# A hybrid decoder layer: TensorE's order in the heads' stage written by hand, in slots between projection matmuls

## The chip, the core and the metric

The kernel runs on one core of one Trainium2 chip. A core has TensorE (PE, matrix products; its weight loads are listed as PEld), VectorE (DVE), ScalarE (ACT), GpSimd (POOL) and SyncE (SP, which here only issues transfers). The metric is the time of one execution on the device in microseconds (us); lower is better.

## What is computed

The reference is one decoder layer on 512 rows of width 2048, all in float32. Cut to what matters:

```python
z = rms_norm(x, g_mix) @ w_in            # [aq | ak | av | rq | rk | rv | rg], 1024 columns each
# group A, 8 heads: causal attention with QK norm and rotary; group B, 8 heads: retention
aq, ak = rotary(rms_norm(aq, q_norm)), rotary(rms_norm(ak, k_norm))
a_out  = softmax(scale * aq @ ak.T + causal) @ av
rq, rk = rotary(rq), rotary(rk) * 128 ** -0.5
r      = (rq @ rk.T * decay[h]) @ rv
r_out  = silu(rg) * rms_norm_per_head(r) * g_ret
x += concat([a_out, r_out]) @ w_o
h2 = rms_norm(x, g_ffn)
x += (silu(h2 @ w_gate) * (h2 @ w_up)) @ w_down
x += (p @ w_ple_proj) * sigmoid(rms_norm(x, g_ple) @ w_ple_gate + b_ple_gate)
```

With two blocks of 256 keys the block selection takes every earlier block, so group A is plain causal attention.

## The kernel before, in words

Every float32 operand is split into a high and a low float32r part (`split`: one ScalarE copy makes the high part `H`, one VectorE subtraction the low part `L`), and a product is three matmuls into one accumulator (`mm3`, lines 62 to 64: H by H, H by L, L by H).

The kernel has three stretches. **First stage** (to about 298 us): `Plain` makes the q and k columns of head pair 0, then three `Group`s make values and gates with a seven-product scheme. One `step` is one unit of 256 rows of weights; `run` walks the steps and extracts (splits) weights two steps ahead. `beside(i)` issues what lies beside step i: loads of chunks of `xT` (`h_chunk`), of the weights `wqk[0]`, and of the first group's weights `w_vg` at steps 2, 3 and 6, four loads at once.

**Heads' stage** (about 298 to 776 us), the one that changes. Heads come in pairs, i = 0 to 3 attention, i = 4 to 7 retention. For each pair the q and k columns are projected by eight units of 24 matmuls (`rows` for attention, `cols` for retention: unit u, then the four accumulators b or f, then two chunks). The four accumulators are the four buffers of the PSUM pool `acc_p`. When a projection is done, `evac` reads each accumulator. For attention it writes `z` (line 606), four squares with sums on ScalarE (line 610), rotary on GpSimd and VectorE, and the normed `z` at line 625. For retention it copies the accumulator to `zr` (line 682), swaps the halves of its partitions by two transfers on ScalarE's queue into `mr` (lines 685, 686), does rotary on VectorE (lines 688 to 690) and splits the result into `qkH`, `qkL`. `zr` and `mr` share four buffers (tag `rm`), which are given out in program order; so do the pieces of `p` (`praw`, line 780) later. `z` and the broadcast `bc` of `load_ropeT` share four buffers (tag `rp`).

Then come the heads: `attend` (transposes of q and k, line 642; scores, softmax; transposes of the weights, line 667; the weighted values, whose copy is line 672) and `retain` (scores times decay, line 713; values, lines 724 and 725; a norm; transposes, line 740; a copy, line 742). The finished pair is turned into the factors of the seven-product scheme (`mixed`), which go straight into a tile `s_o[p]` or through DRAM (`s_mix`). The code asks for pair i's heads before the projection of pair i + 1. The order of every engine's instructions is then laid out by a planner, which walks the program in the order written but lets later instructions go first where earlier ones wait by its own timing; on the chip each engine runs its list in that order and waits where something is not ready.

At the end of the stage the normed input `h` is freed, the tiles `s_o` of four of the seven products take its place and are refilled from DRAM by `back` on ScalarE's queue, and a small projection `w_pp` (four times 24 matmuls) reads `pTH`, split from `praw`. **The rest** (from about 776 us) is `w_o`, the feed-forward part and the gate, all in `Group`s run by `run`.

Of the kernel before, what the change touches and what calls it, by code (L numbers as in the profile page):

```python
# [33 lines left out]
def layer_kernel(ctx, tc, x, xT, pT, g_mix, wqk, w_vg, qk_norm, g_ret, w_ow, g_ffn,  # L34
# [25 lines left out]

    def mm3(o, aH, aL, bH, bL, start, stop, goes_on=False):
        nc.tensor.matmul(o, aH, bH, start=start, stop=False, skip_group_check=goes_on)  # L62
        nc.tensor.matmul(o, aH, bL, start=False, stop=False, skip_group_check=goes_on)  # L63
        nc.tensor.matmul(o, aL, bH, start=False, stop=stop, skip_group_check=goes_on)  # L64
# [16 lines left out]
    def over_partitions(r):  # L81

        tp = tp_p.tile([P, T], F32, name="tp", tag="tp")
        for b in range(NB):
            nc.tensor.transpose(tp[:, b * P:(b + 1) * P], r[:, b:b + 1].to_broadcast([P, P]), ident)
        return tp
# [106 lines left out]
    class Group:  # L193
# [44 lines left out]
        def multiply(self, p, u):  # L238
# [3 lines left out]
            if first:  # L242
                self.bank[k] = [pools["chain"].tile([P, T], F32, name=k + str(b), tag=k + str(b))
                                for b in range(2)]
# [55 lines left out]
    def chunk_of(get, k):  # L300

        tp = tp_p.tile([P, T], F32, name="tp", tag="tp")
        for b in range(NB):
            nc.tensor.transpose(tp[:, b * P:(b + 1) * P], get(b)[:, k * P:(k + 1) * P], ident)
        return tp
# [164 lines left out]
    def beside(i):  # L470
# [30 lines left out]
    acc_p = mix_ctx.enter_context(pool("acc_p", 4, space=PSUM))  # L501
    at_p = mix_ctx.enter_context(pool("at_p", 2, space=PSUM))
# [10 lines left out]
    def weights(src):  # L513
        tags.append(tags.pop(0))
        raw = rawq.tile([P, 2, T], F32, name="raw", tag=tags[0])
        wh = wq.tile([P, 2, T], F32R, name="wh", tag="wh")
        wl = wq.tile([P, 2, T], F32R, name="wl", tag="wl")
        nc.sync.dma_start(raw, src)
        split(wh, wl, raw)
        return wh, wl  # L520

    def rows(units, evac):

        accs = [acc_p.tile([P, T], F32, name="acc", tag="acc") for _ in range(NB)]
        for u, src in enumerate(units):
            wh, wl = weights(src)
            for b in range(NB):
                at = slice(b * P, (b + 1) * P)
                for c in range(2):
                    k = 2 * u + c  # L530
                    H, L = hT[k]
                    mm3(accs[b], H[:, at], L[:, at], wh[:, c, :], wl[:, c, :], k == 0, k == NC - 1)
        for b in range(NB):
            evac(b, accs[b])

    def cols(units, evac):

        accs = [acc_p.tile([P, T], F32, name="acc", tag="acc") for _ in range(4)]
        for u, src in enumerate(units):
            wh, wl = weights(src)  # L540
            for f in range(4):
                at = slice(f * P, (f + 1) * P)
                for c in range(2):
                    k = 2 * u + c
                    H, L = hT[k]
                    mm3(accs[f], wh[:, c, at], wl[:, c, at], H, L, k == 0, k == NC - 1)
        for f in range(4):
            evac(f, accs[f])
# [50 lines left out]
    def qk_attn(i):  # L599
# [33 lines left out]
        else:  # L633
            rows([wqk[i, u] for u in range(NC // 2)], evac)
        return made

    def attend(z, v, j):
        got = []
        for s in range(2):
            tp = tp_p.tile([P, T], F32, name="tp", tag="tp")  # L640
            for b in range(NB):
                nc.tensor.transpose(tp[:, b * P:(b + 1) * P], z[b][:, s, j, :], ident)
            H, L = qk_pair()
            split(H, L, tp)
            got += [H, L]
        qH, qL, kH, kL = got
        PH, PL = p_tiles()
        nc.vector.tensor_scalar(PH[:, 1408:1536], ident, 0.0, None, op0=ALU.mult)
        nc.vector.tensor_scalar(PL[:, 1408:1536], ident, 0.0, None, op0=ALU.mult)
        for qb in range(NB):  # L650
            nk = (qb + 1) * P
            q = slice(qb * P, nk)
            n = max(nk, 256)
            s = at_p.tile([P, T], F32, name="at", tag="at")
            mm3(s[:, :n], qH[:, q], qL[:, q], kH[:, :n], kL[:, :n], True, True)
            nc.vector.tensor_tensor(s[:, q], s[:, q], mask, op=ALU.add)
            mx = stat.tile([P, 1], F32, name="mx")
            nc.vector.tensor_reduce(mx, s[:, :nk], axis=AX.X, op=ALU.max, negate=True)
            nc.vector.tensor_scalar(mx, mx, SCALE, None, op0=ALU.mult)
            pt = ap.tile([P, T], F32, name="pt", tag="pt", bufs=2)  # L660
            sm = stat.tile([P, 1], F32, name="sm")
            nc.scalar.activation(pt[:, :nk], s[:, :nk], AF.Exp, bias=mx, scale=SCALE, accum_out=sm)
            nc.vector.reciprocal(sm, sm)
            nc.vector.tensor_scalar(pt[:, :nk], pt[:, :nk], sm, None, op0=ALU.mult)
            tp = tp_p.tile([P, T], F32, name="tp", tag="tp")
# [92 lines left out]
    for i in range(2 * NPAIR):  # L758
# [4 lines left out]
        if i + 2 != 2 * NPAIR:  # L763
            mixed(i, made)
# [192 lines left out]
```

## Time and profile before

| what | value |
| --- | --- |
| median of 3 runs | 2428.74 us (2426.74 to 2434.04) |
| the profiled execution | 2433.47 us |
| its span, from the first to the last instruction | 2431.7 us |
| PE busy | 2341.2 us, 96% |
| DVE busy | 1957.4 us, 80% |
| ACT busy | 1210.1 us, 50% |

PE's busy time counts matmuls from start to end, and they overlap; a matmul of 512 columns is shown with about 390 ns but the next one starts before it ends. The granted clock (PEclk) is a share of full speed: 1.00 is 2.4 GHz, 0.50 is 1.2 GHz.

### The profile page before, as it was taken

The numbers are of one execution on the slowest core, as the hardware profiler recorded it, in microseconds if no ns is written. First come the engines' busy times: TensorE is split into PE (matmuls) and PEld (weight loads), VectorE is DVE, ScalarE is ACT, GpSimd is POOL, SyncE is SP. The second block draws the span as 40 slices with busy tenths as digits, with TensorE's granted clock in tenths as the row PEclk, the third lists the DMA queues.
The fourth block names the chain that finished last, engine by engine and source line by source line (L and its number), as shares of the span: only waits on it lengthen the run. The fifth ranks groups of instructions, "written<-read, shape, count | busy, mean of one in ns | idle before, by whom it ended". The sixth has DMA issues, their size and how long they took to land.

```text
span 2431.7 us, 29377 instructions
## 1 busy us (share of the span) xinstructions
PE 2341.2 (96%) x10470; PEld 1917.1 (79%) x10470; DVE 1957.4 (80%) x2632; ACT 1210.1 (50%) x1887; POOL 61.8 (3%) x63
## 2 busy tenths in 40 slices
PE   8999999999978998999999999999999999999998
PEld 6788877787867877888888888888878878888777
DVE  6888677766666798789888988889878877789997
ACT  7644534434445565445545554555544433446643
POOL 0000031100000000000000000000000000000000
PEclk9999999998998999999999999999999999999999
DMA  8545633345566766454356434654595676777764
GB/s 321 154 151 189 207 113 117 117 135 157 170 201 242 263 195 270 139 164 141 120 173 191 144 125 145 192 164 137 170 396 171 246 290 208 287 240 240 276 212 121
DMA packets 169283, 467.81 MB, mean 192 GB/s; under 512 B 18736, under 2 KB 31408, under 8 KB 164144
## 3 DMA queue, kind: packets, MB, share of 16 engines
q1 hardware_dynamic: 164992, 455.43, 56.0%
q10 hardware_dynamic: 4144, 10.50, 1.4%
q8 instruction: 82, 1.34, 0.2%
q14 instruction: 65, 0.53, 0.1%
HBM read 356.28 MB, written 105.38 MB: 190 GB/s over the span
## 4 chain that ended last, share of the span: by engine, by line
PE 67%; DVE 9%; DMA 7%; issue 2%; ACT 2%; ACTq 0%; POOL 0%; SPq 0%; DVEq 0%; POOLq 0%
PE Y L63 8%; PE Y L64 8%; PE Y L62 8%; PE Z L63 5%; PE Z L64 5%; PE Z L62 5%; PE X L63 5%; PE X L62 5%; PE X L64 5%; PE acc L62 4%; PE acc L63 4%; PE acc L64 4%; DVE wl L55 3%; DVE raw L70 2%; DMA mr<-zr 2%
## 5 line engine op out<-in xcount | busy, mean ns | idle before, releaser
L54 ACT ACTIVATE wh<-raw 128x1024 fp32r<-128x1024 f32 x726 | 767.5, 1059 | 815.2 <-PE Y L64 287.7
L55 DVE TENSOR_TENSOR wl<-raw,wh 128x1024 fp32r<-128x1024 f32 x726 | 883.7, 1223 | 261.9 <-ACT wh L54 259.8
L70 DVE TENSOR_TENSOR raw<-raw 128x1024 f32<-128x1024 f32 x376 | 455.1, 1223 | 37.6 <-DMA raw<-in_w_gu 15.9
L63 PE MATMUL Y<-wl,s 128*128 128x512 f32 x1080 | 424.7, 393 | 3.2 <-DVE wl L55 3.0
L64 PE MATMUL Y<-wh,s 128*128 128x512 f32 x1080 | 421.1, 390 | 0.0
L62 PE MATMUL Y<-wh,s 128*128 128x512 f32 x1080 | 378.8, 391 | 8.2 <-ACT wh L54 8.2
L63 PE MATMUL Z<-wl,s 128*128 128x512 f32 x752 | 297.8, 396 | 5.2 <-DVE wl L55 5.2
L64 PE MATMUL Z<-wh,s 128*128 128x512 f32 x752 | 294.5, 392 | 0.0
L62 PE MATMUL Z<-wh,s 128*128 128x512 f32 x752 | 265.8, 393 | 2.2 <-DMA s<-h 2.2
L63 PE MATMUL X<-wl,s 128*128 128x512 f32 x656 | 259.0, 395 | 4.8 <-DVE wl L55 4.6
L64 PE MATMUL X<-wh,s 128*128 128x512 f32 x656 | 257.1, 392 | 0.0
L62 PEld LDWEIGHTS Y<-wh,s 128*128 128x128 f32 x1080 | 201.9, 188 | 54.8 <-ACT wh L54 13.2
L63 PEld LDWEIGHTS Y<-wl,s 128*128 128x128 f32 x1080 | 202.7, 188 | 48.1 <-DVE wl L55 6.7
L62 PE MATMUL X<-wh,s 128*128 128x512 f32 x656 | 232.2, 394 | 3.5 <-ACT wh L54 3.5
L64 PEld LDWEIGHTS Y<-wh,s 128*128 128x128 f32 x1080 | 202.9, 188 | 41.0
L63 PEld LDWEIGHTS Z<-wl,s 128*128 128x128 f32 x752 | 142.4, 189 | 38.1 <-DVE wl L55 8.9
L62 PEld LDWEIGHTS Z<-wh,s 128*128 128x128 f32 x752 | 140.9, 189 | 31.8 <-DMA s<-h 2.5
L64 PEld LDWEIGHTS Z<-wh,s 128*128 128x128 f32 x752 | 142.4, 189 | 29.0
L63 PEld LDWEIGHTS X<-wl,s 128*128 128x128 f32 x656 | 124.2, 189 | 33.6 <-DVE wl L55 7.7
L62 PEld LDWEIGHTS X<-wh,s 128*128 128x128 f32 x656 | 124.1, 190 | 30.7 <-ACT wh L54 4.8
L64 PEld LDWEIGHTS X<-wh,s 128*128 128x128 f32 x656 | 124.2, 189 | 25.4
L62 PE MATMUL acc<-h,wh 128*128 128x512 f32 x256 | 101.5, 398 | 4.1 <-ACT zr L682 3.6
(208 smaller groups left out, 2830.3 us busy)
## 6 DMA issues: line engine op xcount, KB each, us to landing
raw<-in_w_gu SPq DMA_DIRECT2D x176, 512.0 KB, 4.3
raw<-in_w_dn SPq DMA_DIRECT2D x88, 512.0 KB, 6.0
a<-o SPq DMA_DIRECT2D x154, 256.0 KB, 2.7
raw<-in_wqk SPq DMA_DIRECT2D x64, 512.0 KB, 3.7
s<-a SPq DMA_DIRECT2D x14, 2048.0 KB, 10.7
raw<-in_w_vg SPq DMA_DIRECT2D x48, 512.0 KB, 5.0
raw<-in_w_ow SPq DMA_DIRECT2D x32, 512.0 KB, 4.3
xin<-x SPq DMA_DIRECT2D x64, 256.0 KB, 5.9
```

The source lines that it names most:

```text
L54: nc.scalar.activation(H, src, AF.Copy)
L55: nc.vector.tensor_tensor(L, src, H.bitcast(F32), op=ALU.subtract)
L62: nc.tensor.matmul(o, aH, bH, start=start, stop=False, skip_group_check=goes_on)
L63: nc.tensor.matmul(o, aH, bL, start=False, stop=False, skip_group_check=goes_on)
L64: nc.tensor.matmul(o, aL, bH, start=False, stop=stop, skip_group_check=goes_on)
L70: nc.vector.tensor_tensor(o, a, b, op=ALU.add)
```

## The change

All matmuls and transposes from the start of the heads' stage to w_o's eighth step are kept in the order in which they are written (`keep_in_program_order`). The order is then written out. A counter `slot` goes up by one before every 12 projection matmuls (`tick`: twice a unit, twice in each quarter of `w_pp`, and once before each of w_o's first steps), and functions registered with `at_slot(n, ...)` run when the counter gets there. `attend` and `retain` no longer do a head; they return its pieces as functions, whose operations are those of before. `heads` puts the pieces of pair i into slots 7 to 18 (attention) or 1 to 15 (retention) after pair i's projection, so into the projection of pair i + 1; those of pair 7 go into `w_pp` and w_o's first steps. The projections of pair 1 to 7 and `w_pp` take their weights from one `stream`, split up to three units ahead. `load_ropeT` stands before pair 4's projection. Pair 6's factors all go through DRAM now. The PSUM of the heads is handed to w_o in two parts: four buffers of `acc_p` to X and Z at w_o's start, two of `at_p` to Y at its step 5. In the first stage the loads of the first group's weights go out one in each step, from steps 3, 6 and 8.

```diff
+    def matmul(*args, **kw):
+        ins = nc.tensor.matmul(*args, **kw)
+        if in_order[0]:
+            tc.keep_in_program_order(ins)
...
-        for at, q in ((2, "11"), (3, "12"), (6, "22")):
-            if i == at:
-                for u in range(4):
-                    groups[0].load(q, u)
+        for at, q in ((3, "11"), (6, "12"), (8, "22")):
+            if at <= i < at + 4:
+                groups[0].load(q, i - at)
...
-    at_p = mix_ctx.enter_context(pool("at_p", 2, space=PSUM))
+    at_p = at_ctx.enter_context(pool("at_p", 2, space=PSUM, side="right"))
+    in_order[0] = True
+    slot = [0]
+    pieces = {}
+    def at_slot(n, fn):
+        pieces.setdefault(slot[0] + n, []).append(fn)
+    def tick():
+        slot[0] += 1
+        for fn in pieces.pop(slot[0], []):
+            fn()
...
+    stream = [wqk[i, u] for i in range(1, 2 * NPAIR) for u in range(NC // 2)] + [w_pp[n] for n in range(NS)]
+    ready = []
+    def weights():
+        while stream and len(ready) < 3:
...
+            split(wh, wl, raw)
+            ready.append((wh, wl))
+        return ready.pop(0)
+    def projection(rows):
         accs = [acc_p.tile([P, T], F32, name="acc", tag="acc") for _ in range(4)]
+        for u in range(NC // 2):
+            wh, wl = weights()
             for f in range(4):
+                if f % 2 == 0:
+                    tick()
...
+    def heads(i, made, v):
+        out = []
+        if i < NPAIR:
+            (turn0, scores0, weights0, result0), (turn1, scores1, weights1, result1) = \
+                [attend(made, v, j) for j in range(2)]
+            plan = ((7, turn0), (8, lambda: scores0((0, 1))), (10, lambda: weights0((0, 1))),
+                    (10, lambda: scores0((2, 3))), (11, turn1), (12, lambda: weights0((2, 3))),
+                    (12, lambda: scores1((0, 1))), (14, lambda: out.append(result0())),
+                    (14, lambda: weights1((0, 1))), (14, lambda: scores1((2, 3))),
+                    (16, lambda: weights1((2, 3))), (18, lambda: out.append(result1())))
+        else:
+            (load0, scores0, normed0, result0), (load1, scores1, normed1, result1) = \
+                [retain(made, v, j, 2 * (i - NPAIR) + j) for j in range(2)]
+            plan = ((1, load0), (5, lambda: scores0((0, 1))), (6, lambda: scores0((2, 3))), (6, load1),
+                    (8, normed0), (9, lambda: scores1((0, 1))), (10, lambda: scores1((2, 3))),
+                    (11, lambda: out.append(result0())), (12, normed1), (15, lambda: out.append(result1())))
+        for n, fn in plan:
+            at_slot(n, fn)
+        at_slot(plan[-1][0], lambda: mixed(i, out))
+
     for i in range(2 * NPAIR):
+        if i == NPAIR:
+            load_ropeT()
+        qk = qk_attn(i) if i < NPAIR else qk_ret(i)
+        heads(i, qk, v_of(i))
+    h_ctx.close()
...
     for n in range(NS):
+        wh, wl = weights()
         accs = [acc_p.tile([P, T], F32, name="acc", tag="acc") for _ in range(NB)]
         for b in range(NB):
+            if b % 2 == 0:
+                tick()
...
+    def take_over(i):
+        if 0 <= i < 10:
+            tick()
+        if i == 5:
+            at_ctx.close()
+            pools["chainY"] = ctx.enter_context(pool("chain3", space=PSUM, side="right"))
+        if i == 8:
+            assert not pieces
+            in_order[0] = False
+            mix_ctx.close()
...
+            for p in "724":
+                nc.sync.dma_start(s_o[p].bitcast(F32), s_mix[p].bitcast(F32))
```

## Rows read from the trace of the kernel before

**Rows 1.** The page: busy time of each engine, with its share of the span and the count of instructions.

```profile
PE 2341.2 (96%) x10470; PEld 1917.1 (79%) x10470; DVE 1957.4 (80%) x2632; ACT 1210.1 (50%) x1887; POOL 61.8 (3%) x63
```

**Rows 2.** PE in order of time at five places: the first projection matmul of the stage, the start of pair 6's projection, the last matmul of pair 7's, the first of w_pp, the first of w_o. Columns: start, length, engine and line, operation, tiles, shape, count, and in brackets idle time before it and what ended that.

```profile
298.32 0.47 PE L62 MATMUL acc<-wh,h 128*128 128x512 f32 x1 [0.38 <-DVE e L67]
...
606.44 0.39 PE L62 MATMUL acc<-h,wh 128*128 128x512 f32 x1
...
715.04 0.39 PE L64 MATMUL acc<-h,wl 128*128 128x512 f32 x1
...
747.37 0.63 PE L62 MATMUL acc<-wh,pT 128*128 128x512 f32 x1
...
775.81 0.40 PE L62 MATMUL X<-wh,s 128*128 128x512 f32 x1
```

**Rows 3.** PE in order of time where nothing holds it up: a head's last matmuls of 384 and 256 columns, four transposes, projection matmuls of 512 columns.

```profile
386.48 0.33 PE L62 MATMUL at<-PH,v 128*128 128x384 f32 x1
387.00 0.28 PE L62 MATMUL at<-PH,v 128*128 128x256 f32 x1
...
387.71 0.60 PE L642 MATMUL tp<-ident,z 128*128 128x128 f32 x4
...
388.38 0.40 PE L62 MATMUL acc<-wh,h 128*128 128x512 f32 x1
...
390.44 0.39 PE L62 MATMUL acc<-wh,h 128*128 128x512 f32 x1
...
392.71 0.39 PE L63 MATMUL acc<-wl,h 128*128 128x512 f32 x1
```

**Rows 4.** PE in order of time at the end of pair 2's projection, up to the start of pair 3's.

```profile
408.19 0.39 PE L64 MATMUL acc<-wh,h 128*128 128x512 f32 x1
...
410.59 0.51 PE L62 MATMUL at<-PH,v 128*128 128x512 f32 x1 [1.25 <-ACT PH L54]
...
416.67 0.79 PE L62 MATMUL acc<-wh,h 128*128 128x512 f32 x1 [0.53 <-ACT m L610]
```

**Rows 5.** Stretches: length, busy time (and count) of PE, PEld, DVE, ACT, POOL, then the granted clock, the share of the DMA engines and GB/s.

```profile
410.00:420.00 10.00, 7.34 (x30) 5.64 (x31) 8.75 (x17) 6.76 (x38) 3.25 (x4) 0.83 0.26 80
470.00:480.00 10.00, 6.68 (x38) 5.09 (x36) 7.37 (x15) 6.76 (x30) 1.58 (x3) 1.00 0.24 75
540.00:570.00 30.00, 22.57 (x90) 17.79 (x89) 21.90 (x54) 13.65 (x31) 0.00 (x0) 0.77 0.42 134
715.00:750.00 35.00, 14.11 (x49) 11.10 (x49) 23.18 (x50) 12.27 (x31) 2.37 (x2) 0.63 0.90 305
400.00:450.00 50.00, 46.68 (x223) 38.38 (x222) 36.46 (x81) 20.56 (x65) 11.80 (x12) 0.97 0.27 85
30.00:35.00 5.00, 0.86 (x4) 0.38 (x2) 0.50 (x1) 0.76 (x2) 0.00 (x0) 0.94 1.03 395
```

**Rows 6.** VectorE in order of time: the first and the last steps of pair 0's `z`.

```profile
309.03 1.29 DVE L606 TENSOR_TENSOR z<-z,sides 128x512 f32<-128x512 f32 x2 [2.61 <-DMA sides<-in_qk_norm]
...
325.01 1.28 DVE L625 TENSOR_TENSOR z<-z,rs 128x512 f32<-128x512 f32 x2
```

**Rows 7.** Groups of instructions from 290 to 760 us: count, busy time and mean ns of one, idle time before.

```profile
L610 ACT ACTIVATE m<-acc 128x128 f32<-128x128 f32 x48 | 12.4, 332 | 0.0
L610 ACT ACTIVATION_READ_ACCUMULATOR m<-acc 128x1 f32 x48 | 11.8, 266 | 0.0
```

**Rows 8.** ScalarE in order of time: the four copies `zr` of pair 5's accumulators.

```profile
600.15 0.60 ACT L682 ACTIVATE zr<-acc 128x512 f32<-128x512 f32 x1 [0.55 <-PE acc L64]
...
603.91 0.60 ACT L682 ACTIVATE zr<-acc 128x512 f32<-128x512 f32 x1
...
610.32 0.58 ACT L682 ACTIVATE zr<-acc 128x512 f32<-128x512 f32 x1
...
616.03 0.58 ACT L682 ACTIVATE zr<-acc 128x512 f32<-128x512 f32 x1
```

**Rows 9.** The chain that ended last, its pieces that are swaps of halves: start, length.

```profile
601.35 6.29 DMA mr<-zr
614.40 4.14 DMA mr<-zr
...
730.01 12.66 DMA mr<-zr
```

**Rows 10.** ScalarE in order of time after pair 7's projection: the first and the third copy `zr`, and the first refill of `s_o`.

```profile
708.98 0.60 ACT L682 ACTIVATE zr<-acc 128x512 f32<-128x512 f32 x1 [0.55 <-PE acc L64]
...
717.28 0.33 ACTq L748 DMA_DIRECT2D s<-mix  x1
...
719.94 0.58 ACT L682 ACTIVATE zr<-acc 128x512 f32<-128x512 f32 x1
```

**Rows 11.** VectorE in order of time: the rotary of pair 7's third accumulator.

```profile
731.41 0.69 DVE L690 TENSOR_TENSOR zr<-zr,mr 128x512 f32<-128x512 f32 x1
```

**Rows 12.** The tile `praw`: its transfers (duration of the issue, first and last start), their time to landing, and, from the waits of SyncE's queue from 700 to 750 us, what its issue waited for.

```profile
L780 SPq DMA_DIRECT2D praw<-in_pT x2: 332/332/333, 736.7 to 741.5; - x2
DMA to landing us min/median/max: 3.4/5.2/7.0
SPq L780 <- DMA s<-mix: 6.0, 2, 4.3
```

**Rows 13.** SyncE's queue in order of time in the first stage.

```profile
16.76 4.92 SPq L204 DMA_DIRECT2D raw<-in_w_vg  x6
```

More of the change, by code (lines that the diff above doesn't have):

```diff
@@ L633, in qk_attn @@
         else:
-            rows([wqk[i, u] for u in range(NC // 2)], evac)
+            for b, acc in enumerate(projection(True)):
+                evac(b, acc)
         return made
     def attend(z, v, j):
[L638 to L645, printed above, removed]
@@ L670, in attend, with turned @@
-        o = weighted(v, (PH, PL), j)
-        a = ev_tile("A", name="o")
-        nc.scalar.activation(a, o, AF.Copy)
-        return a
+        got, pts, ps = [], {}, []
+        def turned():
+            for s in range(2):
+                tp = tp_p.tile([P, T], F32, name="tp", tag="tp")
+                for b in range(NB):
+                    transpose(tp[:, b * P:(b + 1) * P], z[b][:, s, j, :])
+                H, L = qk_pair()
+                split(H, L, tp)
+                got.extend([H, L])
@@ new lines, in weights_turned @@
+        def weights_turned(qbs):
+            if not ps:
+                ps.extend(p_tiles())
+                for t in ps:
+                    nc.vector.tensor_scalar(t[:, 1408:1536], ident, 0.0, None, op0=ALU.mult)
+            PH, PL = ps
+            for qb in qbs:
+                nk = (qb + 1) * P
+                tp = tp_p.tile([P, T], F32, name="tp", tag="tp")
+                for kb in range(qb + 1):
+                    transpose(tp[:, kb * P:(kb + 1) * P], pts[qb][:, kb * P:(kb + 1) * P])
+                blocks = lambda t: t.rearrange("p (k c) -> p k c", c=P)[:, qb:4 * qb + 1:3, :]
+                split(blocks(PH), blocks(PL), tp[:, :nk].rearrange("p (k c) -> p k c", c=P))
@@ L676, in qk_ret, with result @@
+        def result():
+            o = weighted(v, ps, j)
+            a = ev_tile("A", name="o")
+            nc.scalar.activation(a, o, AF.Copy)
+            return a
+        return turned, scores, weights_turned, result
     def qk_ret(i):
@@ L693, in evac @@
             made.append((H, L))
-        cols([wqk[i, u] for u in range(NC // 2)], evac)
+        for f, acc in enumerate(projection(False)):
+            evac(f, acc)
         return made
@@ L738, in retain, with load @@
-        tp = tp_p.tile([P, T], F32, name="tp", tag="tp")
-        for qb in range(NB):
-            nc.tensor.transpose(tp[:, qb * P:(qb + 1) * P], r[:, qb], ident)
-        a = ev_tile("A", name="r")
-        nc.scalar.activation(a, tp, AF.Copy, scale=gr[:, h:h + 1])
-        return a
+        own = {}
+        def load():
+            own["dec"] = ap.tile([P, P + T], F32, name="dec", tag="dec")
+            nc.sync.dma_start(own["dec"], decay_c[h])
+            own["sg"] = rp_tile("sg", (P, NB, HD))
+            nc.sync.dma_start(own["sg"], sgd[:, :, h * HD:(h + 1) * HD])
@@ L746, in back, with result @@
+        def result():
+            tp = tp_p.tile([P, T], F32, name="tp", tag="tp")
+            for qb in range(NB):
+                transpose(tp[:, qb * P:(qb + 1) * P], own["r"][:, qb])
+            a = ev_tile("A", name="r")
+            nc.scalar.activation(a, tp, AF.Copy, scale=gr[:, h:h + 1])
+            return a
+        return load, scores, normed, result
     def back(p, pairs):
         nc.scalar.dma_start(s_o[p][:, pairs].bitcast(F32), s_mix[p][:, pairs].bitcast(F32))
-    qk, v = qk_attn(0), v_of(0)
@@ L884, in layer_kernel, with before @@
     b_at = steps.index((groups[-2], "3", 0))
-    run(lambda i: load_bias() if i == b_at else None)
+    def before(i):
+        take_over(i)
+        if i == b_at:
+            load_bias()
+    run(before)
 def _constants():
```

212 lines of the change are left out of this document (91 added, 121 removed).

## The prediction

> **What bounds the kernel now.** I read the page first: PE is busy 96% of the span [rows 1], so only PE's lost time can be won. Next PE in order of time. With nothing in the way, projection matmuls start 2.27 / 10 = 0.227 us apart, those of 384 columns 0.17, of 256 columns 0.118, and four transposes take 0.67 - 0.227 = 0.44 [rows 3]. At that pace the heads' stage needs: seven projections and w_pp, 1440 matmuls, 327 us; eight attention heads of 18 transposes (2.0) and two products of 3 x (0.227 + 0.17 + 2 x 0.118) = 1.9, so 5.8 each, 46.6; eight retention heads of 1.9 for scores, 20 x 0.118 = 2.4 for values, 0.44 for transposes, 4.7 each, 37.8; four transposes more. Sum 412 us. The stage lasts from 298.32 to 775.81 [rows 2], 477.5 us, so **65.5 us are lost in it**, and that is what this change can work on.
>
> Where? At the ends of the attention projections: between the last matmul at 408.19 and the next projection at 416.67 there are 15 transposes (1.7) and 12 matmuls (1.9), so 8.5 - 0.2 - 3.6 = 4.7 are lost [rows 4], and at this one the granted clock then reads 0.83 over 10 us, 1.7 more; at the third it reads 1.00 [rows 5]. Three such tails: about 17. Around pair 4's rotary table, 540 to 570, 7.4 idle and a clock of 0.77 (up to 6.9 more) [rows 5]: about 14. At the end, from pair 7's last projection matmul at 715.04 to w_pp's first at 747.37 [rows 2], 32.3 us hold 5.7 us of head work: 26.6 lost, and about 2 more at half clock behind it [rows 5]: 28.5. The rest, 6, lies in short waits.
>
> **The change, part by part.** No operation is added or removed, save pair 6's extra way through DRAM (2 MB more, off PE's path). What changes is who waits. An order written by hand never lets a later matmul pass a waiting one; each term below is PE's wait at a place, since every matmul of the stage is queued behind it.
>
> *Tails.* Both heads' pieces lie inside the projection; the last, slot 18, is 1.9 us of work behind the next projection's first 12 matmuls. The tails' 17 go. What comes is the hand-over of accumulators: four squares with sums, 4 x (0.332 + 0.266) = 2.4 us of ScalarE for each accumulator [rows 7]. The first accumulator is done 4.9 us before the projection ends, the four take 9.6, two weight splits of 1.06 lie between, so the last is free some 7 us after the end, and is wanted at 12 + 6 matmuls + 1.9 = 6.0. I take 1.5 for each of three (0 to 4): **4.5**.
>
> *Pair 0.* Its pieces start in slot 7, after three units: 298.32 + 72 x 0.227 = 314.7 [rows 2, 3]. Its last `z` is ready at 325.01 + 1.28 = 326.3, and that chain does not hang on PE: it starts when the table `sides` lands at 309.0 [rows 6]. The planner fed projection matmuls past the transposes there; by hand nothing may pass, so PE waits 11.6, and after such a wait comes a stretch at half clock like the 1.7 above: **13.4** (9 to 15).
>
> *Rotary table.* The 14 go, since the table is made 45 us before it is wanted. But its transposes hold one of two buffers of `tp_p` until `bc` can be written, and `bc` is the fifth user of four `rp` buffers: it waits for pair 3's slot 11. Until then transposes share one buffer; each second one waits for a copy (0.6) and a subtraction (0.69 [rows 11]) and their hand-overs. Two at 1.5, one at 1: **4** (1.5 to 6).
>
> *Retention.* `zr` and `mr` have four buffers, so the third copy waits until the first swap is through. In the trace the third copy starts 10.2 us after the first, the fourth 12.1 after the second [rows 8]; the swap is the larger part of it (6.29 [rows 9]). Before, PE went round this: pair 6's projection started at 606.44 [rows 2] while the third copy came at 610.3. By hand the third accumulator is wanted 2.7 us after the projection's end T. Its first copy starts at T - 3.8 (18 matmuls before the end), so the third is done at T - 3.8 + 10.2 + 0.6 = T + 7.0, a wait of 4.3, and the fourth at T + 10.3 against T + 8.4, 1.9 more: 6.2, and 7.9 with a half-clock stretch. With the shorter swap of 4.14 [rows 9] and VectorE free it is about 2.3. Transfers that ran beside that swap lie elsewhere in the new order, so I take 5.2 for each of three: **15.5** (7 to 24).
>
> *The end.* w_pp's first matmul needs `praw`, whose buffers come after pair 7's third accumulator in the same four. Before, that one's copy started 719.94 - 715.3 = 4.6 after T, its rotary ended at 732.1, 16.8 after T [rows 10, 11], and `praw` was issued at 736.7 and 741.5, SyncE's queue held up 6.0 by refills [rows 12]. The copy came that early because the first accumulator was done at T - 6.3 [rows 10]; now it is T - 3.8, so third copy T + 6.4, rotary T + 18, landing 5.2 later [rows 12], copy and subtraction: w_pp at T + 25, with nothing before it, as its matmuls stand ahead of pair 7's pieces. With half clock after it **27** (21 to 33; the latter if the queue is held as before). So 28.5 become 27. The third swap here runs beside the refills from 717.28 [rows 10], and the fourth took 12.66 against 4.14 in the quiet [rows 9]. The Trainium skill (DMA: Bandwidth & Descriptors, Issuing engines are not separate DMA queues) says that transfers issued by different engines end on the same DMA engines and interleave; the trace agrees, with the 12.66. If the queues were separate, the quiet 4.14 would hold and the end would be 22, the sum 5 lower; I keep 27.
>
> *Slots.* Each piece has one to three slots of 2.7 us behind the one that feeds it. About 80 pieces at 0.06: **5** (2 to 15). *w_o's start*, where pair 7's heads now meet w_o's additions on VectorE: **2** (0 to 8).
>
> *First stage.* Six `w_vg` loads go out at 16.76 in one row [rows 13], with the DMA engines full, and at 30 to 35 PE has 0.86 of 5 us, waiting for `h` [rows 5]; about 8 are lost there. Spread out, the chunks of `xT` come first: **-5.5** (-8 to 0).
>
> Sum of waits: 4.5 + 13.4 + 4 + 15.5 + 27 + 5 + 2 = 71.4, against 65.5; less 5.5: +0.4. So the profiled execution's 2433.5 stays, and since the median lies 4.7 under it, **2429**. The two holes and tails that go (31) are paid back in waits at fixed places.
>
> **The rivals.** *Covered, faster.* The swap is quick without its neighbours (9 for the three instead of 15.5), `praw` comes at T + 20 (22), pair 0 costs 10, slots 2, the table 2, the front gives 7.5: 3 + 10 + 2 + 9 + 22 + 2 + 1 = 49, so 49 - 65.5 - 7.5 = -24: 2405; halfway, about 2412. For: none of the three swaps in rows 9 is typical of a quiet queue except 4.14. Against: pair 0's wait is dated by a load.
>
> *Late pieces, slower.* ScalarE and VectorE still run the planner's order, made by its own timing; each piece that comes late stops PE, where before other matmuls stood in between. VectorE is busy 36.5 of 50 us in this stage [rows 5], and with periods of 57 instead of 61.6 us over 78%. Price: 80 pieces at 0.3 us are 24 instead of 5: 2448. It decides from 0.15 us a piece. Against: PE's whole list of waits before is short.
>
> *The clock.* Short waits in a row at the accumulators throw PE to half clock again and again: half clock followed one tail and not another of the same gaps [rows 5]. At three attention hand-overs, the rest of the retention ones and four slots, 1.7 each: +15, 2444. The Trainium skill (TensorE: Matmul & The Clock Gate, A second HAM failure mode: psum-queue depth-cycling) describes this: micro-idles between groups, as PE goes round its PSUM banks, make the clock swing, and the throughput falls; the 0.83 behind the tail agrees, the 1.00 does not.
>
> **How the numbers follow.** Forecast (even) 0.32; covered 0.33; late pieces 0.27; clock 0.08. What the measurement tells from no change is 0.3%, 7.3 us: faster 0.33 (all of covered), same 0.31, slower 0.36. The forecast's own range is 2419 to 2439; taking in the others, **2407 to 2452**.
>
> **What would show it.** Right: PE waits near 315 for `z` for over 9 us; PE waits on `zr` at the start of the projections of pairs 5 to 7, 2 to 6 us each; no hole at 540 to 570; the projections of attention pairs follow each other with under 2 us lost; nothing on PE for 20 us or more ahead of w_pp. Wrong: w_pp starting within 15 us of pair 7's projection (then some 10 faster), waits of over 0.5 us at most pieces (slower), or a different loss after 860, where I expect none.

## The result

The changed kernel takes 2453.01 us (median of 6 runs, 2444.98 to 2454.19); the kernel before, run beside it, 2432.71 (6 runs). The ratio is **1.0079, with a 95% interval of 1.0059 to 1.0099**: about 19 us slower. My forecast, no change, did not come. Slower came, to which I had given 0.36, against 0.33 for faster and 0.31 for no change. On the 2428.74 from which I forecast, 1.0079 are 2448: outside the forecast's own range (2419 to 2439), near the slow end of the whole one (2407 to 2452). The median itself is 1 us beyond that end, with a kernel before that took 4 us more here.

The page of the changed kernel, to be read against [rows 1]: busy time of each engine. PE's share fell by a point, and its work is the same.

```profile
span 2452.4 us, 29384 instructions
...
PE 2335.7 (95%) x10470; PEld 1914.4 (78%) x10470; DVE 1957.7 (80%) x2632; ACT 1210.5 (49%) x1887; POOL 59.8 (2%) x63
```

PE's waits in the changed heads' stage (290 to 780 us), by line and by what ended them: sum, count, longest. L64 is now every matmul of a product, L69 every transpose.

```profile
PE acc L64 <- ACT pT L54: 31.5, 1, 31.5
PE acc L64 <- ACT zr L720: 11.6, 5, 3.0
PE tp L69 <- DVE z L646: 9.6, 2, 5.3
PE tp L69 <- DVE qkL L55: 5.5, 2, 3.0
PE at L64 <- DVE qkL L55: 2.5, 1, 2.5
PE at L64 <- ACT qkH L54: 1.5, 1, 1.5
```

There are few rows. The first four are fixed places that I had named; the last two, scores that wait for q and k, I had priced only among the slots. Two rows under 1 us follow; all come to 63 us. The same view of the kernel before adds up to 40.

Stretches of the changed kernel that answer to [rows 5]: length, busy time (and count) of PE, PEld, DVE, ACT, POOL, granted clock, DMA share, GB/s.

```profile
310.00:330.00 20.00, 10.27 (x36) 7.81 (x35) 15.18 (x24) 4.70 (x19) 7.80 (x7) 0.66 0.24 75
335.00:485.00 150.00, 149.96 (x750) 126.45 (x749) 118.52 (x278) 69.23 (x215) 34.16 (x36) 1.00 0.38 120
490.00:525.00 35.00, 28.83 (x133) 23.57 (x132) 19.39 (x47) 12.50 (x28) 0.00 (x0) 0.90 0.41 128
540.00:570.00 30.00, 23.68 (x100) 18.67 (x99) 21.14 (x38) 11.18 (x20) 0.00 (x0) 0.94 0.64 187
660.00:690.00 30.00, 25.79 (x101) 20.40 (x100) 21.05 (x35) 12.38 (x21) 0.00 (x0) 0.83 0.52 148
725.00:770.00 45.00, 13.53 (x51) 10.57 (x50) 16.58 (x28) 12.33 (x23) 0.00 (x0) 0.66 0.80 283
```

For 150 us, over three attention hand-overs, PE never stops and its clock reads 1.00. That is what the change was good for. Before and behind it stand the holes.

To add this up I take the length of a stretch less the matmuls that start in it, each at its pace [rows 3] (0.227 us for 512 columns, 0.176 for 384, 0.118 for 256, 0.114 for a transpose). The paces are rounded here; by them a cell comes out up to 0.7 lower, differences between kernels hardly change. This lost time holds waits and half clock alike. Here it is for all kernels; the experiments follow below.

```
lost us   pair 0   attention  table    hand-overs  end      then
          290-335  335-485    485-525  525-700     700-780  780-1010
before      2.1      17.5       0.1      17.8 (a)    29.3     16.9
after      13.9       1.2       9.7      26.3        34.2     17.2
e_free      1.4      13.7       0.2      16.1        27.8     16.6
e_front    13.0       1.2       8.3      24.0        36.3     16.7
e_pair0     0.8      10.5       9.9      24.0        33.6     17.0
e_bc       12.3       1.4       0.6      24.5        33.8     17.9
e_zr       13.2       1.4       8.3      22.0        27.8     17.0
e_late     13.7       1.4       9.8      26.2        26.4     16.7
e_ret3     14.1       1.2       8.8      16.9        29.4     16.6
e_end      12.8       1.2       8.3      22.3        25.6     18.2
e_hbest     3.1      13.8       0.8      15.6        24.9     16.2
e_fbest     3.0      10.1       0.3       3.6        21.5     23.0
e_fback     2.1      11.2       0.2      14.9        31.1     14.1
e_spread    1.9       8.5       0.2       6.6        12.7     23.0
(a) 14.6 of it is the rotary table's hole, 525 to 580
```

Before to after: 66.8 lost become 85.3 from 290 to 780, +18.5. The first stage gives 1.8 (23.4 to 21.6 lost), which is within what the traces differ by (see e_front). Of the profile's 20.7 us of difference 4 lie elsewhere: some 6 more are lost behind 2000 us, some 2 fewer between 1010 and 2000.

### The profile page after: what moved, and what is told of

Read it like the earlier page. It is cut to its first block, busy times and chain, and to the rows that moved or that the text cites. A ratio compares the mean times of both kernels' runs of the same rounds, so it can differ in the third digit from the quotient of the medians.

```text
span 2452.4 us, 29384 instructions
## 1 busy us (share of the span) xinstructions
PE 2335.7 (95%) x10470; PEld 1914.4 (78%) x10470; DVE 1957.7 (80%) x2632; ACT 1210.5 (49%) x1887; POOL 59.8 (2%) x63
## 4 chain that ended last, share of the span: by engine, by line
PE 66%; DVE 11%; DMA 7%; issue 2%; ACT 1%; ACTq 0%; SPq 0%; DVEq 0%
PE Y L64 22%; PE Z L64 15%; PE X L64 14%; PE acc L64 11%; DVE wl L55 4%; DVE raw L82 3%; PE at L64 3%; PE tp L69 2%; DMA h<-o 1%; DMA mr<-zr 1%; DMA xin<-x 1%; DVE t L79 1%; ACT wh L54 1%; DMA mix<-o 1%; DVE o L55 1%
## 5 line engine op out<-in xcount | busy, mean ns | idle before, releaser
L64 PE MATMUL Y<-wh,s 128*128 128x512 f32 x2160 | 680.9, 391 | 7.2 <-ACT wh L54 7.2
L64 PEld LDWEIGHTS Y<-wh,s 128*128 128x128 f32 x2160 | 405.3, 188 | 94.0 <-ACT wh L54 11.0
L64 PE MATMUL Z<-wh,s 128*128 128x512 f32 x1504 | 475.0, 391 | 2.3 <-DMA s<-h 2.1
L64 PE MATMUL Y<-wl,s 128*128 128x512 f32 x1080 | 425.2, 394 | 3.5 <-DVE wl L55 3.3
L64 PE MATMUL X<-wh,s 128*128 128x512 f32 x1312 | 416.8, 393 | 5.3 <-ACT wh L54 5.3
L64 PEld LDWEIGHTS Z<-wh,s 128*128 128x128 f32 x1504 | 282.3, 188 | 60.7 <-DMA s<-h 2.3
L64 PE MATMUL Z<-wl,s 128*128 128x512 f32 x752 | 297.4, 396 | 6.2 <-DVE wl L55 6.2
L64 PEld LDWEIGHTS X<-wh,s 128*128 128x128 f32 x1312 | 248.1, 189 | 58.4 <-ACT wh L54 7.2
L64 PE MATMUL X<-wl,s 128*128 128x512 f32 x656 | 259.1, 395 | 5.8 <-DVE wl L55 5.7
L64 PEld LDWEIGHTS Y<-wl,s 128*128 128x128 f32 x1080 | 203.2, 188 | 48.4 <-DVE wl L55 7.3
L64 PE MATMUL acc<-h,wh 128*128 128x512 f32 x512 | 166.3, 407 | 11.6 <-ACT zr L720 11.6
L64 PEld LDWEIGHTS Z<-wl,s 128*128 128x128 f32 x752 | 141.7, 188 | 40.7 <-DVE wl L55 12.4
L64 PEld LDWEIGHTS X<-wl,s 128*128 128x128 f32 x656 | 124.1, 189 | 34.4 <-DVE wl L55 8.8
L64 PE MATMUL acc<-wh,h 128*128 128x512 f32 x384 | 124.9, 396 | 0.4 <-DVE e L79 0.4
L64 PEld LDWEIGHTS acc<-h,wh 128*128 128x128 f32 x512 | 98.2, 197 | 33.1 <-ACT zr L720 14.0
L64 PE MATMUL acc<-h,wl 128*128 128x512 f32 x256 | 103.2, 403 | 0.0
L64 PEld LDWEIGHTS acc<-wh,h 128*128 128x128 f32 x384 | 73.2, 191 | 15.8 <-issue 0.8
L54 ACT ACTIVATE o<-t 128x256 fp32r<-128x256 f32 x149 | 56.6, 409 | 45.3 <-DVE t L79 35.6
L64 PE MATMUL acc<-wl,h 128*128 128x512 f32 x192 | 75.7, 394 | 0.0
```

What stands on the lines that cost most here:

```text
L54: nc.scalar.activation(H, src, AF.Copy)
L64: ins = nc.tensor.matmul(*args, **kw)
```

## The experiments

My theory was that each hole has a cause of its own, a wait that the order written by hand cannot go round. The rival was that the lost time is conserved: that another engine or the transfers set it, and it comes back at the next place. Every ratio is to the kernel before on the same chip.

**e_free: the slots without the order.** One line goes.

```diff
-    in_order[0] = True
```

> The changed kernel with its slots, streams and pools, but the tensor engine's order in the heads' stage left to the planner instead of held as written. Theory (the order held by hand makes the engine stand at a late piece, pair 0 and the hand-overs of pairs 4 to 6, with projection matmuls ready behind it): the loss of 13 us in pair 0 and of 25 at the hand-overs shrinks to a third or less, the end stays at 30 or more, time 2425 to 2438. Rival (the waits come from buffers and latencies that any order meets): the same places lose as much, time 2449 to 2456.

Measured: 2430.07 us, 0.9983 (0.9974 to 0.9993). Its four longest rows of waits from 290 to 780:

```profile
PE at L64 <- ACT qkH L54: 28.5, 4, 23.0
PE acc L64 <- ACT zr L719: 2.8, 1, 2.8
PE acc L64 <- DVE wl L55: 2.4, 1, 2.4
PE tp L69 <- DVE qkL L55: 1.9, 2, 1.4
```

The theory's time came. The slots, streams and pools with the planner's order are as fast as the kernel before, 0.2% faster; **keeping the order by hand costs 1.0079 - 0.9983, about 23 us**. The waits on `z` and most of those on `zr` are gone, since PE goes round them. In detail it is not as I wrote: the hand-overs of pairs 4 to 6 still lose 16 of 26, the end falls to 27.8, and the attention hand-overs lose 13.7 again, against 1.2. The order by hand wins 12.5 there and loses 12.5 in pair 0, 9.5 at the table, 10 at the hand-overs and 6 at the end. One reservation: with that line gone the planner lays out the lists of ScalarE and VectorE anew too (in the two traces they run in a different order), so the 23 us are the price of the fixed order together with what the planner makes of the rest; no run parts the two.

**e_front: the first stage's loads as before**, all else changed.

```diff
-        for at, q in ((3, "11"), (6, "12"), (8, "22")):
-            if at <= i < at + 4:
-                groups[0].load(q, i - at)
+        for at, q in ((2, "11"), (3, "12"), (6, "22")):
+            if i == at:
+                for u in range(4):
+                    groups[0].load(q, u)
```

> The changed kernel with the loads of w_vg of the first stage back at the steps where the kernel before has them, all four at once. Theory (these loads gave 1.8 us of the 5.5 that I forecast): projection 1 starts 1 to 3 us later than at 296.5, time 2453 to 2457. Rival (the moved loads gave the 5.5 and something else in the first stage took the rest): projection 1 starts 4 to 7 us later, 2457 to 2460.

Measured: 2448.59, 1.0063 (1.0045 to 1.0081), no slower than with the new loads, and projection 1 starts 0.4 us later. Both fail: no gain from the moved loads can be told. With the new loads the first stage loses between 21.6 and 24.3 us in the traces here, with the old ones 22.0 and 23.4.

**e_pair0: pair 0's pieces five slots later.**

```diff
+        held = 5 if i == 0 else 0
         for n, fn in plan:
-            at_slot(n, fn)
+            at_slot(n + held, fn)
```

> The changed kernel with pair 0's twelve pieces held five slots later and nothing else. Theory (pair 0's z are late for their slot, and the stall and the clock behind it cost 13.4 us between 310 and 330): both waits on z go, the tensor engine keeps full clock there, and the time falls by 9 to 13 us, to 2440 to 2444 (1.003 to 1.005 of before). Rival (the lost time is only moved: pair 0's last pieces now meet pair 1's first in projection 2, and vector and scalar engine are no earlier with them): waits of the same size on tiles of pair 0 or 1 between 340 and 380, time 2449 to 2455.

Measured: 2448.02, 1.0065 (1.0043 to 1.0088); by the times alone not to be told from the changed kernel. The trace is clear: 13.1 us go at the old place and 9.3 come back in the next 150. PE's waits there, 310 to 400:

```profile
PE at L64 <- ACT pt L686: 4.5, 1, 4.5
PE tp L69 <- DVE pt L688: 1.4, 2, 0.8
PE tp L69 <- DVE qkL L55: 0.8, 1, 0.8
```

Five slots later, pair 0's softmax falls into the hand-over of projection 1. The engine behind the longest of these waits is VectorE, not ScalarE, which had made the squares by then and stood idle for VectorE's maximum `mx`:

```profile
356.86 0.37 ACT L686 ACTIVATE pt<-at,mx 128x128 f32<-128x128 f32 x1 [2.86 <-DVE mx L683]
```

From 340 to 370 VectorE is busy for 26.64 of 30 us, with the norm and rotary of projection 1's `z` among it. For this hole the rival is right, for some two thirds of it.

**e_bc: the broadcast row in a buffer of its own.**

```diff
-        bc = rp_tile("bc")
+        bc = ap.tile([P, 2, T], F32, name="bc", tag="pT")[:, 0, :]
```

> The changed kernel with the broadcast row bc in a buffer of its own (the pT tile's, idle until the end), nothing else. Theory (bc waits for a buffer of the z of pair 3, so one of the two tp tiles is held and the transposes of head 0 wait, 9.8 us with the clock between 490 and 525): the two waits of the transposes on qkL go, the loss there falls to 1 to 3 us, time down by 6 to 9, to 2444 to 2447. Rival (the transposes wait for the vector engine's split itself, not for the buffer): the waits stay, time 2451 to 2455.

Measured: 2443.83, 1.0053 (1.0038 to 1.0067). The two waits are gone, and where the clock read 0.90 (above) this stretch now shows

```profile
490.00:525.00 35.00, 34.74 (x178) 29.27 (x177) 24.76 (x65) 15.49 (x36) 0.00 (x0) 1.00 0.48 152
```

The loss falls from 9.7 to 0.6 and does not come back: theory. The time is just below the theory's, and its interval overlaps that of the changed kernel; it is the trace that decides.

**e_zr: copies 2 and 3 of each retention projection elsewhere**, in the idle pT tile.

```diff
-            z = rm_tile("zr")
+            if f == 2:
+                late.append(ap.tile([P, 2, T], F32, name="zr", tag="pT"))
+            z = rm_tile("zr") if f < 2 else late[0][:, f - 2, :]
```

> The changed kernel with the last two of the four copies zr of each retention projection in the idle pT tile instead of the four rm buffers. Theory (the hand-overs cost 8 to 9 us each, 25 together, because copies 2 and 3 wait for the buffers of 0 and 1, hold the accumulators, and the tensor engine falls to half clock): the five waits of acc on zr (11.6 us) go, the hand-overs shrink to 2 to 5 us each, and the time falls by 10 to 18, to 2435 to 2443. Rival (the scores wait for q and k, which the swaps' latency sets): the wait moves from the accumulators to at or tp on qkH or qkL in the next slots, time 2448 to 2455.

Measured: 2443.07, 1.0049 (1.0029 to 1.007). PE's waits from 525 to 705, over the three hand-overs:

```profile
PE at L64 <- DVE qkL L55: 7.4, 3, 3.7
PE at L64 <- ACT qkH L54: 4.6, 2, 2.6
PE acc L64 <- ACT zr L723: 0.3, 1, 0.3
```

The accumulators' waits went from 11.6 to 0.3 and the scores' waits on q and k from 4.0 to 12.0: the rival's transfer, to the letter. The hand-overs lose 22.0 instead of 26.3, not the theory's 6 to 15. The time is at the slow edge of the theory's all the same, since most of it was won elsewhere, at the end (27.8 instead of 34.2), where `praw` no longer comes behind those copies in the same four buffers.

**e_ret3: on top of e_zr, the pieces later**: pairs 4 and 5 by three slots, pair 6 by one.

```diff
+        held = {4: 3, 5: 3, 6: 1}.get(i, 0)
```

> The kernel of e_zr (copies 2 and 3 in the pT tile), and the pieces of pairs 4 and 5 three slots later, those of pair 6 one slot later. Theory (with the accumulators free, slot 5 is too early for the first scores: q and k come some 9 us later than their slot): the waits of at on qkH and qkL go at the hand-overs of pairs 4 and 5 (near 550 and 610), where 5 to 7 us each are lost in e_zr, down to 1 or 2 us, and shrink by less than half at that of pair 6; time 8 to 12 below e_zr's 2443, 2431 to 2435. Rival (the vector engine is the limit: each hand-over's loss is its backlog, and comes back at a later slot): waits of the same sum between 550 and 600 and between 610 and 660, time 2440 to 2445.

Measured: 2439.01, 1.0028 (1.0016 to 1.0041); some 4 us won, not 8 to 12. By stretch, e_zr's losses 6.2, 7.6 and 8.2 (525 to 580, 580 to 640, 640 to 700) become 1.7, 4.4 and 10.8. At pair 4 no wait on q or k is left. At pair 5 what is left is a wait of 2.1 for a weight. At pair 6, moved by one slot only, there stand

```profile
PE at L64 <- ACT qkH L54: 4.8, 1, 4.8
PE at L64 <- DVE qkL L55: 2.3, 1, 2.3
```

Where the pieces moved three slots the loss shrank by 4.5 and 3.2, with no such wait at a later slot of the same projection; there the theory holds for the mechanism. Of these 7.7 us the third hand-over lost 2.6 again and the end 1.6. Whether more than one slot would have mended the third was not tried.

**e_late: the refills of w_o's factors behind the last swap** on ScalarE's queue.

```diff
+            swap[0] = nc.scalar.dma_start(m[half:], z[:half])
...
+        with tc.issue_after(swap[0].ins):
+            nc.scalar.dma_start(s_o[p][:, pairs].bitcast(F32), s_mix[p][:, pairs].bitcast(F32))
```

> The changed kernel with the refills of w_o's factor tiles queued on the scalar engine behind the last swap of pair 7, nothing else. Theory (seven refills of half a megabyte each, issued from 731 on, hold ACT's queue and the DMA engines, so the third swap goes out at 738.5 instead of 733 and lands in 8 instead of 4 us): w_pp's first matmul comes 6 to 12 us earlier than 759, time 2441 to 2447, if the refills are not needed sooner. Rival (they are: w_o's first steps wait for them): w_pp starts earlier, but X or Z wait for s after it by as much, time 2450 to 2458.

Measured: 2441.87, 1.0045 (1.0029 to 1.006). The chain at the end, changed kernel first, then e_late: start, length, what.

```profile
731.67 6.69 DMA mix<-o
...
738.46 0.47 ACTq L723
...
739.00 8.13 DMA mr<-zr
...
748.55 0.70 DVE zr L728
...
749.30 9.12 DMA praw<-in_pT
...
759.13 13.19 PE acc L64 x48
```

```profile
728.74 4.24 DMA mix<-o
...
738.13 2.44 DMA mr<-zr
...
741.99 0.70 DVE zr L730
743.10 8.49 DMA s<-mix
751.99 0.64 ACT pT L54
752.67 14.20 PE acc L64 x48
```

The swap lands in 2.44 us instead of 8.13, PE's wait falls from 31.5 to 22.5, and nothing comes back behind it. So the refills stretched the swap, and the theory's time came. The third swap was issued less early than I had written: at 737.6 here, which is 7.4 us behind projection 7's end (730.2) instead of 10.8. And now the refills hold the queue ahead of pT's split.

**e_end: on top of e_zr, pT loaded and split during projection 7.**

```diff
+    def load_pT():
+        for k in range(2):
+            both = [rp_tile("pT", dt=F32R) for _ in range(2)]
...
+            raw = ap.tile([P, T], F32, name="praw", tag="pt", bufs=2)
+            nc.sync.dma_start(raw, pT[k * P:(k + 1) * P, :])
+            split(*both, raw)
...
+        if i == 2 * NPAIR - 2:
+            plan += (13, load_pT),
```

> The kernel of e_zr, and pT loaded and split during projection 7, into the four rp buffers that the heads of pair 6 have left, so that w_pp waits neither for the rm buffers nor for the loads; sg of pair 7 then comes after w_pp. Theory (the hole at the end is the chain of the last q and k, the loads of pT behind it and their split; w_pp itself needs none of it): w_pp's first matmul within 3 us of projection 7's last, the 27 us lost there in e_zr fall to 5 to 15 (the scores of pair 7 and the refills of w_o are next in the order), time 12 to 22 below e_zr, 2421 to 2431. Rival (the refills set the end: w_o cannot start before its factors are in, and they start only when h is done with): the tensor engine waits as long after w_pp instead, for s from the refills, time 2438 to 2445.

Measured: 2440.78, 1.0043 (1.0031 to 1.0054), 2 us under e_zr instead of 12 to 22. The hole only changed its name. PE's waits from 715 to 800, and below them ScalarE's queue in order of time:

```profile
PE acc L64 <- ACT pp L871: 17.3, 4, 8.9
```

```profile
735.71 11.20 ACTq L806 DMA_DIRECT2D s<-mix  x8
746.95 0.63 ACT L54 ACTIVATE qkH<-zr 128x512 fp32r<-128x512 f32 x1 [10.67 <-DMA s<-mix]
```

w_pp starts at once, but its accumulators are emptied by ScalarE, which for 11 us issues refills. The rival's time came, by another way than it said: not w_o waits, but ScalarE. That its queue is what sets the end does not follow from this trace, as e_hbest shows next.

**e_hbest, e_fbest, e_fback: the fixes together.** e_hbest joins e_bc, e_zr and e_end, `held = {0: 3, 4: 3, 5: 3, 6: 1}`, and issues the refills from GpSimd; e_fbest is the same without the order by hand; e_fback is e_free with GpSimd's refills alone.

```diff
-        nc.scalar.dma_start(s_o[p][:, pairs].bitcast(F32), s_mix[p][:, pairs].bitcast(F32))
+        nc.gpsimd.dma_start(s_o[p][:, pairs].bitcast(F32), s_mix[p][:, pairs].bitcast(F32))
```

> Order still held by hand, with the edits of the earlier runs together (bc in the pT tile, copies 2 and 3 of zr there too, pieces of pairs 0, 4 and 5 three slots later and of pair 6 one, pT loaded and split during projection 7) and the refills of w_o's factors issued from GpSimd's queue. Theory (each of the losses has its own cause, and at the end it is the refills' issue that holds the scalar engine's queue for 11 us in e_end): pair 0 loses 7 instead of 13 us, the tables 1 instead of 10, the hand-overs 12 to 15 instead of 25, the end 10 to 15 instead of 34; sum 45 to 50, so 2403 to 2410. Rival (w_o cannot start before its factors are in, whoever issues them): the end keeps 25 or more, waits of X on s, 2420 to 2428.

> The kernel of e_hbest with the tensor engine's order left to the planner. Theory (with buffers and refills out of the way little is left to wait for, and the planner's order fills it): 10 to 25 us below e_free's 2430, 2405 to 2420, within 6 us of e_hbest. Rival (the planner's own estimates place its holes, and they do not go with these buffers): the losses at the hand-overs near 340, 400, 460 and 540 and at the end stay, 2425 to 2432.

> The kernel of e_free (planner's order) with the refills of w_o's factors on GpSimd's queue, nothing else. Theory (the refills' issue holds the scalar engine's queue at the end): the 27 us lost there fall to 15 to 21, time 2418 to 2425. Rival (their transfers are the limit, not their queue): 2427 to 2432.

Measured: e_hbest 2428.81, 0.9992 (0.9982 to 1.0001); e_fbest **2407.94, 0.9903 (0.9889 to 0.9918)**; e_fback 2425.74, 0.998 (0.9971 to 0.999). Waits of e_hbest from 310 to 420, and the two longest rows of e_fbest from 290 to 800:

```profile
PE tp L69 <- DVE pt L688: 9.3, 3, 6.2
PE tp L69 <- DVE z L646: 1.8, 2, 1.5
```

```profile
PE acc L64 <- ACT pp L871: 12.2, 5, 4.8
PE at L64 <- ACT qkH L54: 4.3, 2, 2.2
```

With equal buffers the order by hand again costs 21 us: the planner's order leaves 3.6 us at the hand-overs, the hand's 15.6, and pair 0 moved by three slots loses 13.8 in the next stretch, as much as it ever did. The theory's sum for e_hbest failed there (7 expected) and at the end (24.9, with 10 to 15 expected), and I had expected e_fbest within 6 us of it. At the end, with the refills off ScalarE's queue, PE waits for `pp` as long as in e_end:

```profile
PE acc L64 <- ACT pp L872: 17.3, 4, 10.5
```

So that queue was not the limit. The chain of e_hbest runs through a write `mix<-o` (11.38 us), the third swap (9.20, from 725.20) and its rotary to the copy of `pp` at 737.08, and `pp` takes its buffers from the same four as the swaps' `mr`. In e_fbest and e_spread the last column of the table is 6 higher, which I have not followed up. For e_fback neither range was met (2418 to 2425, 2427 to 2432), but the rival's mechanism holds: with the refills on another queue the ratio is that of e_free (0.998 and 0.9983), and the end loses 31.1 against 27.8.

**e_spread: half the refills later**, those of tiles 6 and 3 behind the last write of pp, on top of e_fbest.

```diff
-        nc.gpsimd.dma_start(s_o[p][:, pairs].bitcast(F32), s_mix[p][:, pairs].bitcast(F32))
+        q = nc.gpsimd if p in "15" else nc.sync
+        q.dma_start(s_o[p][:, pairs].bitcast(F32), s_mix[p][:, pairs].bitcast(F32))
...
+            wrote = nc.sync.dma_start(ppd[b][:, n], t)
...
+    with tc.issue_after(wrote.ins):
+        for n in range(NS):
+            back("6", slice(2 * n, 2 * n + 2 if n < 3 else 7))
+        back("3", slice(0, 7))
```

> The kernel of e_fbest with half of the refills (tiles 6 and 3 of w_o's factors) issued by SyncE behind the last write of pp, instead of all of them as soon as h's space is free. Theory (at the end the DMA engines are full for some 30 us, share 0.97 to 1.04 from 690 to 730, and that stretches the small transfers which the tensor engine waits for, a swap to 8.6 and a write of pp to 12 and 8 us): with half the traffic gone from there the swaps and writes come down to 4 to 6 us, the waits of acc on pp from 12 to under 5 us, time 2398 to 2404. Rival (the chain over the buffers sets the end, not the traffic, or Y and Z now wait for the late refills): waits of the same sum, or of s, 2405 to 2412.

Measured: **2404.55, 0.9882 (0.986 to 0.9905)**, the fastest here, between the theory's time and the rival's; its interval overlaps e_fbest's. The end's waits, 690 to 820, and one stretch of e_fbest, then of e_spread:

```profile
PE acc L64 <- ACT pp L872: 8.8, 3, 6.9
```

```profile
710.00:720.00 10.00, 8.02 (x27) 6.27 (x28) 6.37 (x12) 4.22 (x10) 1.64 (x3) 0.77 1.04 393
```

```profile
710.00:720.00 10.00, 8.27 (x31) 6.42 (x30) 5.87 (x13) 4.90 (x11) 0.00 (x0) 0.82 0.73 251
```

The DMA engines are no longer full there, and PE waits 8.8 for `pp` instead of 12.2, not under 5. The end loses 8.8 us less than in e_fbest, but the hand-overs lose 3 more and the time behind 2000 us 7 more (see below), and the two profiles are only 3 us apart. The swaps did not come down (one still takes 8.50 at 696.55). How much of the end is traffic and how much the chain over the buffers stays open.

## Where the prediction held and where it failed, point by point

Most mechanisms were those that I had listed, and the sum over them was too low: 71.4 forecast, 85.3 measured. Retention cost 10.8 more than forecast, the end 7.2, the table 5.7, pair 0 0.5; tails, slots and w_o's start together 10.3 less; and the 5.5 of the first stage did not come. That the ratio came to the 2448 of the rival *late pieces* is luck: neither that rival nor *the clock* is what happened. Term by term:

- *Pair 0*, 13.4 forecast: 13.9. The place and the cause are right; that the size is, is partly luck, since 9.6 were waited instead of 11.6, and 4.3 went besides instead of 1.8. PE in order of time, to be read with [rows 6]:

```profile
317.53 0.47 PE L69 MATMUL tp<-ident,z 128*128 128x128 f32 x1 [4.32 <-DVE z L646]
323.29 1.93 PE L69 MATMUL tp<-ident,z 128*128 128x128 f32 x6 [5.28 <-DVE z L646]
```

- *Tails, hand-overs and slots*, 4.5 + 5 forecast: 1.2. Here I was too high for attention: from 335 to 485, with all pieces of pairs 1 and 2, PE waits for none. The late pieces of the stage outside pair 0 and the table are retention's first scores (4.0, below) and a transpose (0.7). Over 80 pieces that is 0.06 us each, as I gave, and the rival **late pieces**, which decided from 0.15, is out.
- *Rotary table*, 4 forecast, bound 6: 9.7. The step was right (one `tp` buffer held behind `bc`, as e_bc shows) and its size was wrong. I took two waits of 1.5 and one of 1; they were 2.96 and 2.51, with 0.7 for a third, and behind both of the long ones the clock fell, which this term left out (0.67 from 495 to 500, 0.72 from 515 to 520):

```profile
497.30 1.11 PE L69 MATMUL tp<-ident,z 128*128 128x128 f32 x4 [2.96 <-DVE qkL L55]
498.07 1.20 PE L64 MATMUL acc<-h,wh 128*128 128x512 f32 x2
...
516.35 0.66 PE L69 MATMUL tp<-ident,z 128*128 128x128 f32 x4 [2.51 <-DVE qkL L55]
```

- *Retention*, 15.5 forecast, bound 24: 26.3. At the accumulators 11.6 were waited, under 4 for each of three, about what I gave. One step I did not take: the first scores stand in slot 5, and I had them among 80 pieces at 0.06 us, when q and k come by the same late copies and swaps. They waited 4.0, nearly all that I gave for every slot of the stage. At pair 4's hand-over three waits follow one another:

```profile
549.44 0.74 PE L64 MATMUL acc<-h,wh 128*128 128x512 f32 x2 [2.10 <-ACT zr L720]
...
558.11 0.50 PE L64 MATMUL at<-qkH 128*128 128x512 f32 x1 [1.53 <-ACT qkH L54]
...
561.39 0.69 PE L64 MATMUL at<-qkH,qkL 128*128 128x512 f32 x1 [2.55 <-DVE qkL L55]
```

  Waits come to 15.6 over the three hand-overs. The rest of the 26.3, 3.6 for each instead of the 1.7 that I gave, is for the most part half clock behind them: the clock reads 0.66 from 560 to 565 and from 615 to 620, and 0.54 from 670 to 680. These waits are also why one of my signs failed, no hole at 540 to 570: the rotary table's is gone, and 6.3 us are idle there for pair 4's hand-over.
- *The end*, 27 forecast, 33 "if the queue is held as before": 34.2. T is 727.7. The third copy came at T + 4.6, earlier than my T + 6.4, but its swap went out at T + 10.8 and took 8.13 us, its rotary ended at T + 21.6 instead of T + 18, and `praw` took 9.12 to land instead of 5.2 [rows 12]. What I had called off PE's path, pair 6's way through DRAM, is in this chain: the swap's issue follows a write `mix<-o`, in the chain above. e_late shows that the refills stretch the swap. I had weighed the Trainium skill here (DMA: Bandwidth & Descriptors, Issuing engines are not separate DMA queues), by which transfers interleave on the same DMA engines whichever engine issues them, and the runs bear it out: e_fback, with the refills on GpSimd's queue, is no faster than e_free (0.998 and 0.9983).
- *First stage*, -5.5 forecast: nothing, by e_front. The step took the six loads at 16.76 for what `h` waits for at 30 to 35, and they were not: a hole of 3.8 us is still there at 36.
- *w_o's start*, 2 forecast: nothing; 780 to 1010 loses 17.2 against 16.9.
- *A different loss after 860*, of which I expected none: 4 us in the profiles. From 2000 us on the kernel before and e_fbest lose 26, all the others here 28 to 33, whatever their edit. No run tells why; it stays open.

The rival **the clock** is not it either. The lost time that is no wait was 27 us before (66.8 less 40) and is 22 now; all of the growth is in waits. In this stage the clock fell only behind the waits listed above, and not behind each: from 545 to 560, with waits of 2.10 and 1.53, it reads 1.00. The Trainium skill (TensorE: Matmul & The Clock Gate, A second HAM failure mode: psum-queue depth-cycling) has the clock swing where PE idles briefly and often as it goes round its PSUM banks; over the three attention hand-overs PE went round four accumulators without such gaps (busy 149.96 of 150 us) and the clock reads 1.00, so that case did not arise.

Taken as a whole: I wrote that two holes and tails of 31 us would be paid back in waits at fixed places. They were, 1.6 times over. In the kernel before, the planner's order went round pair 0's `z` and two of the three hand-overs at little loss; the price of not going round is what e_free shows. And of theory and rival in the experiments neither holds throughout: the table's hole had a cause of its own (e_bc), while pair 0's loss moved to the next hand-over (e_pair0) and the accumulators' waits to the scores (e_zr).

## What to carry to other kernels

An order written by hand is worth its slots only where the operands are early: before fixing one, list for each piece the latest arrival of its inputs and the buffers that they queue for, and price the first piece behind each hand-over by itself, not as one of many. A piece that is late in the trace is not always mended by a later slot alone, since the next hand-over may be there (e_pair0, e_hbest); free the buffer or shorten the chain first (e_bc). And when the planner's order with the new structure is one line away, run it: here it was 0.2% faster than the kernel before, and with the buffers freed 1.0 to 1.2%. The freed buffers were not tried in the kernel before, so how much of that needs the slots is open.

## What I had not expected of the hardware

A swap of 128 KB landed in 2.44 us when the refills were held behind it and in 8.13 beside them. Issuing them can itself hold an engine: eight issues kept ScalarE's queue for 11.20 us in e_end, and the next activation came when one of these transfers had landed; yet with them on GpSimd's queue (e_hbest) the end lost 24.9 against 25.6. And a wait cost more than its length: 13.9 us were lost in pair 0 for 9.6 us of waiting, in a stretch whose granted clock reads 0.66.
